# The grouped norm of a decoder trunk: summing squares onto all partitions with a matrix of ones, and taking the reciprocal root there

## The chip, the cores and the metric

The kernel runs on one core of a Trainium2 chip. The core has five engines that work side by side, each through its own instructions in order: TensorE (PE in the profile; its weight loads are a row of their own, PEld), VectorE (DVE), ScalarE (ACT), GpSimd (POOL) and SyncE (SP), which issues most of the DMAs. The metric is the device time of one execution in microseconds (us), the median of several runs.

## The reference

Two layers of a hybrid decoder, on a sequence of 256 tokens with 1024 channels in float32. Each layer normalises its input, makes one wide projection of it, and runs three token mixers on the parts: a Mamba-2 scan, a sliding-window attention and a forgetting attention. Each mixer has a SiLU gate; its result is projected back to 1024 channels, the three are merged with sigmoid gates, and an output projection is added to the stream.

The change touches the end of the Mamba branch, the grouped norm, which takes the mean of squares over each of 4 groups of 256 channels, per token:

```python
def grouped_rms_norm(y, w, groups):
    b, s, d = y.shape
    yf = y.astype(jnp.float32).reshape(b, s, groups, d // groups)
    yf = yf * lax.rsqrt(jnp.mean(yf * yf, axis=-1, keepdims=True) + NORM_EPS)
    return (yf.reshape(b, s, d) * w.astype(jnp.float32)).astype(y.dtype)

    y = y.reshape(b, s, SSM_INNER) * jax.nn.silu(z)     # the end of mamba2_branch
    return grouped_rms_norm(y, norm_w, SSM_GROUPS)
```

## The kernel before

**Layout.** In the Mamba branch the channels lie on the 128 partitions and the 256 tokens along the row. `y.xs` holds 8 such tiles of 128x256, so a group of the norm is two tiles, and its sum of squares runs over two tiles and all 128 partitions, for each of 256 columns.

**Products in two halves.** A large product is made with operands split into a high part, rounded to the matmul's fast float32r format, and the low rest: high times high, low times high and high times low are added in PSUM. The helper `split` (L291, L292) makes both parts: an ACT copy to the high part and a DVE subtraction for the low one. Every weight that arrives from memory goes through it as two pieces of 128x1024 a block (`hi`, `lo`), so DVE and ACT must keep ahead of PE with weights all the time. `AHEAD` pieces at most are held split.

**The order of work.** PE's order is written by hand: the kernel is recorded under a manual schedule for PE, unit after unit (a unit is one projection of 128 channels, or of 512 columns for one half of the tokens). After a unit, and at some points within, `pump` lets small generators, such as a norm group, take a step. A generator's step is due a given time after the last, by a planner's clock that counts matmuls (L101 to L110): `D_GN1` is 8.0 us from launch to the first visit to PE, `D_GN2` 13.5 us from there to the second. DVE, ACT and POOL get their order from a scheduler that follows dependencies and priorities; in the program that is built it is fixed. What is in the list `ends_later` is recorded behind the next eviction of a product out of PSUM (`finish`).

**The norm, before.** In `u_z` (L863 to L902) the gate of tile `u` is made (`gated`, L876 and L877) and multiplied in (L888); the tile is squared on ACT (L890). After each second tile the two squares are added (L893) and a generator `group_norm` is launched. It does, per group:

1. first visit to PE: the squares (two blocks of 128 tokens) as the weights and two columns of ones as the moving operand, so that the sums come out with the tokens on partitions: 4 used columns in PSUM;
2. on DVE `v`, mean and epsilon (L909, 128x4); on POOL the power -1/2 (L912, 128x4);
3. on DVE a Newton step in three operations (L917, L918, L920), and the split into high and low (L923, L924); on ACT four diagonal matrices, identity times the value of each token (L927);
4. second visit to PE: a matrix of ones times these diagonals, which leaves the value of each token on all partitions, 128x256 in PSUM;
5. for both tiles the product with the norm's weight and this value (L940), and its split into the operands of the projection (`y.yh`, `y.yl`).

**Around it.** While the four groups of a layer go through this, PE works on the last units of the gate, on value products of an attention (L676 evicts them), and on the 512-column sigmoid gates (L1022 evicts them). The branch's projection follows, whose first piece needs the first groups' results and whose second the last group's. POOL's next work behind the four powers is the merge of the projected branch (L1070).

The lines that the instructions of the norm carry in the changed kernel: square sum L894, `v` L914, power L915, Newton step L919 (twice) and L920, product L929.

Of the kernel before, what the change touches and what calls it, by code (L numbers as in the profile page):

```python
# [11 lines left out]
F32 = mybir.dt.float32  # L12
F32R = mybir.dt.float32r
AF = mybir.ActivationFunctionType
ALU = mybir.AluOpType

P = 128
S = 256
# [4 lines left out]
EPS = 1e-6  # L23
# [3 lines left out]
D_GN1, D_GN2, D_CUM, D_H, D_M = 8.0, 13.5, 12.0, (4.8, 6.4), 5.0  # L27
# [20 lines left out]
def hybrid_trunk(  # L48
# [5 lines left out]
    nc = tc.nc  # L54
# [11 lines left out]
    def T(tag, shape, dtype=F32, bufs=None):  # L66
        count[0] += 1
        return sb.tile(shape, dtype, tag=tag, name=f"{tag}_{count[0]}",
                       bufs=bufs if bufs is not None else BUFS.get(tag, 1))

    def PS(tag, bufs):
        count[0] += 1
        return ps.tile([P, 512], F32, tag=tag, name=f"{tag}_{count[0]}", bufs=bufs)
# [4 lines left out]
    def pmx():  # L78
        return PS("mx", 5)

    act = nc.scalar.activation
    stt = nc.vector.scalar_tensor_tensor
    tt = nc.vector.tensor_tensor
    ts = nc.vector.tensor_scalar
    gtt = nc.gpsimd.tensor_tensor
# [14 lines left out]
    def mm(o, a, b, **kw):  # L100
        n = b.free_size()  # L101
        if a.dtype == F32R:
            clock["t"] += max(0.094, n / 2350.0)
        else:
            clock["t"] += max(0.2, n / 587.0) * (0.5 if a.free_size() == 64 or a.shape[0] == 32 else 1.0)
        nc.tensor.matmul(o, a, b, **kw)  # L106
# [5 lines left out]
    def launch(br, gen, delay=0.0):  # L112
        clock["n"] += 1
        waiting.append([clock["t"] + delay, clock["n"], br, gen, None, False])
# [32 lines left out]
    def pump(budget=BUDGET):  # L147
        t0 = clock["t"]
        half = False
        while True:  # L150
            over = clock["t"] - t0 >= budget
            if over and not half:
                return
            for m in sorted(waiting, key=lambda m: (m[0], m[1])):
                if ready(m) and (m[5] if over else not early(m)):
                    half = m[5]
                    enter(m)
                    break
            else:
                return  # L160

    def drain(br):

        left = 0
        while any(m[2] == br for m in waiting):
            for m in sorted(waiting, key=lambda m: (m[0], m[1])):
                if m[2] == br and allowed(m):
                    left += 1
                    enter(m)
                    break  # L170
            else:
                m = min((m for m in waiting if allowed(m)), key=lambda m: (m[0], m[1]))
                left += 1
                enter(m)
        if left and VERBOSE:
            print("drained", br, left, "at", round(clock["t"], 1))
# [10 lines left out]
    ident = T("ident", [P, P])  # L187
# [11 lines left out]
    onesr = T("ones", [P, P], F32R)  # L199
    nc.gpsimd.tensor_copy(onesr, one)  # L200
    ones = onesr.bitcast(F32)
# [9 lines left out]
    mhalf = T("mhalf", [P, 8])  # L211
# [11 lines left out]
    def root(v, n):  # L223
        r0 = T("sm", [P, 8])
        nc.gpsimd.tensor_tensor(r0[:, :n], v[:, :n], mhalf[:, :n], op=ALU.pow)
        return r0
# [54 lines left out]
    def halves(ap):  # L281

        return ap.rearrange("p (a i) -> p a i", a=2)
# [4 lines left out]
    def split(hi, lo, src, scale=None, keep=lambda f: f):  # L288

        if scale is None:  # L290
            keep(act)(hi, src, AF.Copy)  # L291
            keep(tt)(lo, src, hi.bitcast(F32), op=ALU.subtract)  # L292
        else:
            keep(act)(hi, src, AF.Copy, scale=scale)
            keep(stt)(lo, src, scale, hi.bitcast(F32), op0=ALU.mult, op1=ALU.subtract)
# [130 lines left out]
    for l in range(L):  # L426
        y = Layer()
# [49 lines left out]
    def chan_sum(y, w, c, out):  # L477


        p = pmm()  # L480
        both_sums(y, w, c, p)
        finish(act(halves(out), ordered(p[:, S:2 * S]), AF.Copy))
        tt(halves(out), ordered(p[:, 0:S]), halves(out), op=ALU.add)

    def dma_sum(y, w, c, out):

        p = pmm()
        both_sums(y, w, c, p)
        lo = T("L1", [P, S])
        act(halves(lo), ordered(p[:, S:2 * S]), AF.Copy)  # L490
        last = act(halves(out), ordered(p[:, 0:S]), AF.Copy)  # L491
        nc.gpsimd.dma_start(out, lo, accum_op=ALU.add)  # L492
        finish(last)

    def after_evictions(n, f):

        ends_later.append(f if n == 1 else lambda: after_evictions(n - 1, f))
# [298 lines left out]
    ends_later = []  # L796
# [68 lines left out]
    def u_z(y, br, u, c):  # L865
        def f(w):
            if u == 0 and br != 0:
                y.sz[br] = T("L8", [P, NK, S])
            elif u == 0:
                y.yh[br] = T("L8", [P, 2, NK, P], F32R)  # L870
                y.yl[br] = T("L8", [P, 2, NK, P], F32R)
            o = T("L1", [P, S]) if br == 0 else y.sz[br][:, u, :]

            def gated():
                th = T("L1", [P, S])
                act(th, o, AF.Tanh, scale=0.5)  # L876
                stt(o, th, 1.0, o, op0=ALU.add, op1=ALU.mult)  # L877
                y.zdone.add((br, u))
            if br == 1:
                dma_sum(y, w, c, o)  # L880
                after_evictions(3, gated)
                pump()
                return
            chan_sum(y, w, c, o)

            def normed():
                gated()
                tt(y.xs[:, u, :], y.xs[:, u, :], o, op=ALU.mult)  # L888
                sq = T("L1", [P, S])
                act(sq, y.xs[:, u, :], AF.Square)  # L890
                y.sq.append(sq)
                if u % 2 == 1:
                    tt(y.sq[-2], y.sq[-2], y.sq[-1], op=ALU.add)  # L893
                    launch(3 if u < 4 else 4, group_norm(y, u // 2, y.sq[-2]), D_GN1)  # L894
            if br == 0:
                drain(0)

                ends_later.append(normed)
            else:
                gated()  # L900
            pump()
        return f  # L902

    def group_norm(y, g, q0):
        p = pmx()
        for t in range(2):
            mm(p[:, 2 * t:2 * t + 2], q0[:, t * P:(t + 1) * P], ones[:, 0:2], start=True, stop=True)
        v = T("sm", [P, 8])
        ts(v[:, 0:4], p[:, 0:4], 1.0 / 256, 4 * EPS, op0=ALU.mult, op1=ALU.add)  # L909

        r0 = T("sm", [P, 8])
        nc.gpsimd.tensor_tensor(r0[:, 0:4], v[:, 0:4], mhalf[:, 0:4], op=ALU.pow)  # L912
        rbs = [T("L1", [P, S], F32R) for _ in range(2)]

        def diagonals():  # L915
            a = T("sm", [P, 8])
            tt(a[:, 0:4], r0[:, 0:4], v[:, 0:4], op=ALU.mult)  # L917
            tt(a[:, 0:4], a[:, 0:4], r0[:, 0:4], op=ALU.mult)  # L918
            r = T("rs", [P, 8], bufs=4)  # L919
            stt(r[:, 0:4], a[:, 0:4], -3.0, r0[:, 0:4], op0=ALU.add, op1=ALU.mult)  # L920

            rh, rl = T("sm", [P, 8], F32R), T("sm", [P, 8])
            nc.vector.tensor_copy(rh[:, 0:4], r[:, 0:4])  # L923
            tt(rl[:, 0:4], r[:, 0:4], rh[:, 0:4].bitcast(F32), op=ALU.subtract)  # L924
            for rb, v_ in zip(rbs, (rh.bitcast(F32), rl)):
                for t in range(2):
                    act(rb[:, t * P:(t + 1) * P], ident, AF.Copy, scale=v_[:, 2 * t:2 * t + 1])  # L927


        ends_later.append(diagonals)  # L930
        yield D_GN2
        if diagonals in ends_later:
            ends_later.remove(diagonals)
            diagonals()
        p = pmx()
        for i, rb in enumerate(rbs):
            mm(p[:, 0:S], onesr, rb, start=(i == 0), stop=(i == 1))
        for u in (2 * g, 2 * g + 1):
            n = T("L1", [P, S])
            stt(n, y.xs[:, u, :], y.vec[:, 80 + u:81 + u], p[:, 0:S], op0=ALU.mult, op1=ALU.mult)  # L940
            split(y.yh[0][:, :, u, :], y.yl[0][:, :, u, :], halves(n))


# [255 lines left out]
    for y in layers:  # L1199
# [10 lines left out]
        def cols(c0, n=256):  # L1210
            return sub([(0, w[:, c0:c0 + n])], n)
# [39 lines left out]
        if l == 0:  # L1251
            v, cv0, cv1 = cols(C_BV), cols(C_CV), cols(C_CV + 256)
# [8 lines left out]
        else:  # L1261
            cv0, v = cols(C_CV, 512), cols(C_BV)
# [87 lines left out]
    with tc.manual_schedule(engines={ENG.PE, ENG.DVE, ENG.Activation, ENG.Pool}):  # L1350
# [11 lines left out]
        p = pmx()  # L1362
# [93 lines left out]
        for i in range(2):  # L1456
# [4 lines left out]
        v = T("sm", [P, 8])  # L1461
        nc.vector.tensor_reduce(v[:, 0:2], ss.rearrange("p (t j) -> p t j", t=2), axis=mybir.AxisListType.X,
                                op=ALU.add)
        ts(v[:, 0:2], v[:, 0:2], 1.0 / D, EPS, op0=ALU.mult, op1=ALU.add)
        r0 = root(v, 2)
# [48 lines left out]
```

## Time and profile before

| | |
|---|---|
| median of 3 runs | 821.57 us (821.18 to 821.93) |
| profiled execution | 820.72 us, its span 819.0 us |
| mean granted clock of TensorE | 0.999 |
| busy: PE / DVE / ACT / POOL | 808.4 / 671.5 / 547.6 / 172.6 us |
| first-layer norm | `v` of the first group at 297.0 us, last product L940 ends at 333 us |
| second-layer norm | last `v` at 719.5 us |

The span runs from the first instruction to the last in one execution that the hardware profiler recorded; the rest of the execution's time lies around it. A row of a group gives the line, engine, operation, what it writes and reads with shapes, how often, then total busy time and the mean of one in ns, then idle time of the engine before these instructions and what ended it. A row of the timeline gives start and duration in us, and in brackets the idle time before and who ended it. A row of the waits gives who waited for whom: total us, times, longest. A row of stages gives busy time of each engine in a window. The chain is followed back from the last instruction, at each step to what released it.

### The profile page before, as it was taken

What the parts mean: (1) busy time and instruction counts of PE and PEld (TensorE: products, weight loads), DVE (VectorE), ACT (ScalarE), POOL (GpSimd) and SP (SyncE); (2) the same over time, 40 slices, a digit from 0 to 9 for tenths busy, and PEclk for the clock granted to TensorE, in tenths of its full rate; (3) what the DMA queues carried; (4) which work ended last, traced back from release to release, by engine and by line L of the source; (5) the groups of instructions that cost most, each with busy time, mean ns of one, the idle gap of its engine ahead of it and who ended that gap; (6) DMA issues with size and microseconds to landing.
All of it is one profiled execution on the core that took longest, in us unless ns stands there. A gap on an engine that the chain in (4) does not pass through costs nothing.

```text
span 819.0 us, 15070 instructions
## 1 busy us (share of the span) xinstructions
PE 808.4 (99%) x5242; PEld 721.2 (88%) x5242; DVE 671.5 (82%) x1468; ACT 547.6 (67%) x1186; POOL 172.6 (21%) x232
## 2 busy tenths in 40 slices
PE   8999999999999999999999999999999999999996
PEld 8998988888888988888999898889888889888896
DVE  6879899888998787965786989988899878787665
ACT  7777878775776767543666777886567767684452
POOL 3066113130210001030005621314004210102100
PEclk9999999999999999999999999999999999999999
DMA  9897869797865554866689787869868565467632
GB/s 312 278 261 193 211 187 256 190 233 214 232 206 157 180 168 148 276 208 205 221 265 265 186 222 206 228 179 259 243 206 231 155 181 163 137 208 265 206 104 77
DMA packets 141653, 170.35 MB, mean 208 GB/s; under 512 B 9314, under 2 KB 110298, under 8 KB 141578
## 3 DMA queue, kind: packets, MB, share of 16 engines
q1 hardware_dynamic: 114960, 140.53, 54.8%
q0 software_dynamic: 12928, 12.63, 9.5%
q10 hardware_dynamic: 13690, 16.24, 6.5%
q8 instruction: 41, 0.67, 0.3%
q14 instruction: 34, 0.28, 0.1%
HBM read 154.63 MB, written 2.16 MB: 191 GB/s over the span
## 4 chain that ended last, share of the span: by engine, by line
PE 85%; DVE 4%; DMA 4%; ACT 4%; issue 2%; POOL 0%; SPq 0%; ACTq 0%; DVEq 0%; POOLq 0%
PE mm L106 75%; PE mx L106 7%; PE mx L110 3%; DMA L<-cumd 2%; DVE lo L292 1%; ACT hi L291 1%; DVE L L781 1%; ACT pp L621 1%; DMA L<-L 1%; DMA raw<-in_w_in_dram 1%; DMA bias<-cumd 1%; ACT L L778 0%; ACT L L490 0%; DVE L L830 0%; POOL bias L991 0%
## 5 line engine op out<-in xcount | busy, mean ns | idle before, releaser
L292 DVE TENSOR_TENSOR lo<-raw,hi 128x1024 fp32r<-128x1024 f32 (+2 forms) x276 | 310.5, 1144 | 53.2 <-ACT hi L291 50.5
L106 PE MATMUL mm<-L,hi 128*128 128x512 f32 x1056 | 353.2, 386 | 0.0
L106 PE MATMUL mm<-hi,L 128*128 128x512 f32 (+2 forms) x1232 | 323.3, 351 | 0.1
L291 ACT ACTIVATE hi<-raw 128x1024 fp32r<-128x1024 f32 (+2 forms) x276 | 263.9, 981 | 57.2 <-PE mm L106 45.2
L106 PE MATMUL mm<-L,lo 128*128 128x256 f32 x1056 | 266.6, 273 | 0.0
L106 PEld LDWEIGHTS mm<-hi,L 128*128 128x128 f32 x1232 | 216.9, 190 | 24.1 <-issue 1.3
L106 PEld LDWEIGHTS mm<-L,hi 128*128 128x128 f32 x1056 | 194.5, 190 | 26.4 <-issue 3.2
L106 PE MATMUL mm<-lo,L 128*128 128x512 f32 (+2 forms) x616 | 213.8, 349 | 1.8 <-DVE lo L292 1.8
L106 PEld LDWEIGHTS mm<-L,lo 128*128 128x128 f32 x1056 | 202.1, 191 | 5.5
L106 PEld LDWEIGHTS mm<-lo,L 128*128 128x128 f32 x616 | 116.3, 190 | 14.1 <-DVE lo L292 2.6
L492 POOL DMA_DIRECT2D L<-L x68 | 59.4, 925 | 184.5 <-ACT L L491 151.3
L621 ACT ACTIVATE pp<-pp,nm 128x128 f32<-128x128 f32 (+1 forms) x128 | 56.5, 442 | 30.8 <-DVE nm L615 30.7
L991 POOL TENSOR_SCALAR_AFFINE_SELECT bias<-bias 128x128 f32<-128x128 f32 x64 | 34.6, 592 | 93.5 <-DMA bias<-cumd 92.7
L781 DVE SCALAR_TENSOR_TENSOR L<-L,vec,L 128x255 f32<-128x255 f32 (+2 forms) x96 | 46.2, 481 | 2.2 <-ACT L L778 0.5
L490 ACT ACTIVATE L<-mm 128x256 f32<-128x256 f32 x84 | 31.6, 376 | 15.9 <-PE mm L106 14.2
L1025 ACT ACTIVATE L<-L 128x512 f32<-128x512 f32 x24 | 15.1, 629 | 31.6 <-DVE L L1022 27.2
L633 DVE TENSOR_SCALAR pp<-pp,rsum 128x128 f32<-128x128 f32 (+1 forms) x128 | 32.5, 319 | 0.5
L492 POOL DMA_DIRECT2D qt<-L x16 | 14.5, 990 | 81.9 <-ACT qt L491 40.4
L877 DVE SCALAR_TENSOR_TENSOR L<-L,L 128x256 f32<-128x256 f32 x48 | 21.4, 449 | 8.6 <-ACT L L876 8.3
L652 ACT ACTIVATE L<-mx 128x512 f32<-128x512 f32 x48 | 26.8, 595 | 1.5 <-PE mx L110 1.5
L1070 POOL TENSOR_TENSOR L<-L,L 128x512 f32<-128x512 f32 x8 | 12.8, 1598 | 68.4 <-DVE L L1069 68.4
L912 POOL TENSOR_TENSOR sm<-sm,mhalf 128x4 f32<-128x4 f32 x8 | 8.1, 1019 | 90.5 <-DVE sm L909 90.5
(197 smaller groups left out, 841.8 us busy)
## 6 DMA issues: line engine op xcount, KB each, us to landing
raw<-in_w_in_dram SPq DMA_DIRECT2D x191, 512.0 KB, 4.7
raw<-in_w_proj_dram SPq DMA_DIRECT2D x48, 512.0 KB, 5.3
L<-L POOLq DMA_DIRECT2D x72, 128.0 KB, 5.0
raw<-in_w_out_dram SPq DMA_DIRECT2D x16, 512.0 KB, 5.1
bias<-cumd ACTq DMA_DIRECT2D x16, 256.0 KB, 3.4
L<-cumd ACTq DMA_DIRECT2D x8, 512.0 KB, 5.9
L<-in_gate_bias_dram ACTq DMA_DIRECT2D x12, 256.0 KB, 5.9
qt<-L POOLq DMA_DIRECT2D x16, 128.0 KB, 5.6
```

What stands on the lines that cost most here:

```text
L106: nc.tensor.matmul(o, a, b, **kw)
L110: nc.tensor.transpose(o, a, i)
L291: keep(act)(hi, src, AF.Copy)
L292: keep(tt)(lo, src, hi.bitcast(F32), op=ALU.subtract)
L490: act(halves(lo), ordered(p[:, S:2 * S]), AF.Copy)
L492: nc.gpsimd.dma_start(out, lo, accum_op=ALU.add)
L621: act(pp[:, i, sl], pp[:, i, sl], AF.Exp, scale=-1.0, bias=nm[:, e:e + 1], accum_out=sums[:, e:e + 1])
L633: ts(pp[:, i, sl], pp[:, i, sl], rs[:, 2 * i + b:2 * i + b + 1], 0.5, op0=ALU.mult, op1=ALU.mult)
L652: act(pT, pt, AF.Copy)
L781: stt(a[:, s:S], x_[:, 0:S - s], y.vec[:, 16 * j + u:16 * j + u + 1], a[:, s:S], op0=ALU.mult, op1=ALU.add)
L877: stt(o, th, 1.0, o, op0=ALU.add, op1=ALU.mult)
L991: nc.gpsimd.affine_select(out=bias[:, i, dst], in_=bias[:, i, src], compare_op=ALU.is_ge, fill=NEG, base=0, pattern=[[-1, P]], channel_mul ...
```

## The change

The squares of a group are added as before, but the sum is then split into high and low parts (`parts_`). The first visit multiplies a matrix of ones as the weights by these two parts, so that the sum of each token comes out on all 128 partitions at once, 128x256. `v`, the power on POOL and the Newton step now work on 128x256 instead of 128x4; the exponent is one column, broadcast along the row. Diagonals and the second visit to PE are gone; the products with the norm's weight read the value from SBUF. The due times are unchanged.

```diff
                 if u % 2 == 1:
-                    tt(y.sq[-2], y.sq[-2], y.sq[-1], op=ALU.add)
-                    launch(3 if u < 4 else 4, group_norm(y, u // 2, y.sq[-2]), D_GN1)
+                    q = y.sq[-2]
+                    tt(q, q, y.sq[-1], op=ALU.add)
+                    parts_ = [T("L1", [P, S], F32R) for _ in range(2)]
+                    split(*parts_, q)
+                    launch(3 if u < 4 else 4, group_norm(y, u // 2, parts_), D_GN1)
...
-    def group_norm(y, g, q0):
+    def group_norm(y, g, parts_):
         p = pmx()
-        for t in range(2):
-            mm(p[:, 2 * t:2 * t + 2], q0[:, t * P:(t + 1) * P], ones[:, 0:2], start=True, stop=True)
-        v = T("sm", [P, 8])
-        ts(v[:, 0:4], p[:, 0:4], 1.0 / 256, 4 * EPS, op0=ALU.mult, op1=ALU.add)
-        r0 = T("sm", [P, 8])
-        nc.gpsimd.tensor_tensor(r0[:, 0:4], v[:, 0:4], mhalf[:, 0:4], op=ALU.pow)
-        rbs = [T("L1", [P, S], F32R) for _ in range(2)]
-        def diagonals():
-            a = T("sm", [P, 8])
-            tt(a[:, 0:4], r0[:, 0:4], v[:, 0:4], op=ALU.mult)
-            tt(a[:, 0:4], a[:, 0:4], r0[:, 0:4], op=ALU.mult)
-            r = T("rs", [P, 8], bufs=4)
-            stt(r[:, 0:4], a[:, 0:4], -3.0, r0[:, 0:4], op0=ALU.add, op1=ALU.mult)
-            rh, rl = T("sm", [P, 8], F32R), T("sm", [P, 8])
-            nc.vector.tensor_copy(rh[:, 0:4], r[:, 0:4])
-            tt(rl[:, 0:4], r[:, 0:4], rh[:, 0:4].bitcast(F32), op=ALU.subtract)
-            for rb, v_ in zip(rbs, (rh.bitcast(F32), rl)):
-                for t in range(2):
-                    act(rb[:, t * P:(t + 1) * P], ident, AF.Copy, scale=v_[:, 2 * t:2 * t + 1])
-        ends_later.append(diagonals)
+        for i, q in enumerate(parts_):
+            mm(p[:, 0:S], onesr, q, start=(i == 0), stop=(i == 1))
+        v, r = T("L1", [P, S]), T("L1", [P, S])
+        ts(v, p[:, 0:S], 1.0 / 256, 4 * EPS, op0=ALU.mult, op1=ALU.add)
+        gtt(r, v, mhalf[:, 0:1].to_broadcast([P, S]), op=ALU.pow)
+
+        def newton():
+            for _ in range(2):
+                tt(v, v, r, op=ALU.mult)
+            stt(r, v, -3.0, r, op0=ALU.add, op1=ALU.mult)
+
+        ends_later.append(newton)
         yield D_GN2
-        if diagonals in ends_later:
-            ends_later.remove(diagonals)
-            diagonals()
-        p = pmx()
-        for i, rb in enumerate(rbs):
-            mm(p[:, 0:S], onesr, rb, start=(i == 0), stop=(i == 1))
+        if newton in ends_later:
+            ends_later.remove(newton)
+            newton()
         for u in (2 * g, 2 * g + 1):
             n = T("L1", [P, S])
-            stt(n, y.xs[:, u, :], y.vec[:, 80 + u:81 + u], p[:, 0:S], op0=ALU.mult, op1=ALU.mult)
+            stt(n, y.xs[:, u, :], y.vec[:, 80 + u:81 + u], r, op0=ALU.mult, op1=ALU.mult)
             split(y.yh[0][:, :, u, :], y.yl[0][:, :, u, :], halves(n))
```

## The prediction

> **What bounds the kernel now.** I read the page first (busy shares, then the chain that ended last), then the busy time by stage around the grouped norm, then the waits, and last the single instructions of the norm on POOL, DVE and PE. The page:
>
> ```profile
> span 819.0 us, 15070 instructions
> ...
> PE 808.4 (99%) x5242; PEld 721.2 (88%) x5242; DVE 671.5 (82%) x1468; ACT 547.6 (67%) x1186; POOL 172.6 (21%) x232
> ...
> PE 85%; DVE 4%; DMA 4%; ACT 4%; issue 2%; POOL 0%; SPq 0%; ACTq 0%; DVEq 0%; POOLq 0%
> ```
>
> TensorE (PE) is the bound: busy 99%, and 85% of the chain. POOL is busy 21% and has no share of the chain. The stage of the first layer's norm, with its columns PE, weight loads, DVE, ACT, POOL, then clock and DMA:
>
> ```profile
> 297.00:327.00 30.00, 30.00 (x171) 26.05 (x170) 23.05 (x59) 21.15 (x47) 4.04 (x4) 1.00 0.50 159
> ```
>
> PE has no gap in these 30 us, DVE is idle for 7 of them. A matmul saved here shortens the run, and so does nothing else; but DVE feeds PE (it makes the `lo` half of every weight and adds the results out of PSUM), so a DVE that stands still stops PE some microseconds later. The waits between POOL and DVE in the norm, in total over both layers:
>
> ```profile
> POOL sm L912 <- DVE sm L909: 90.5, 6, 29.1
> ...
> DVE sm L917 <- POOL sm L912: 7.0, 6, 1.2
> ```
>
> The first row is POOL without work. The second is what matters: DVE already stands still for each power, 1.2 us at most, because the Newton step stands right behind it in DVE's order. Today PE does not feel it.
>
> **The change part by part.** *The power on POOL.* Four times a layer, the power (L912) on 128x4 becomes one on 128x256 with a broadcast exponent. No power that wide is in the trace. The powers that are:
>
> ```profile
> L912 POOL TENSOR_TENSOR sm<-sm,mhalf x8: 1001/1008/1056, 297.2 to 719.8; 128x4 f32<-128x4 f32 x8
> ...
> L258 POOL TENSOR_TENSOR sm<-sm,mhalf x2: 577/1024/1471, 404.0 to 414.6; 128x1 f32<-128x1 f32 x2
> ...
> L225 POOL TENSOR_TENSOR sm<-sm,mhalf x1: 713/713/713, 15.3 to 15.3; 128x2 f32<-128x2 f32 x1
> ```
>
> (min/median/max in ns.) One column takes 577 ns, two 713, four 1008: 136 ns more for the second column, 147.5 for each of the next two. A line through them is 430 ns and 144 ns a column, which at 256 columns is 37.3 us; by the two slopes, 1.008 + 252 x 0.136 = 35.3 and 1.008 + 252 x 0.1475 = 38.2 us. Against it stands the other single-column power, 1471 ns: with it the mean of one column is that of four, and one could say that the width costs nothing. And the same op slot with an addition or a subtraction:
>
> ```profile
> L1070 POOL TENSOR_TENSOR L<-L,L 128x512 f32<-128x512 f32 x8 | 12.8, 1598 | 68.4 <-DVE L L1069 68.4
> ...
> L565 POOL TENSOR_TENSOR L<-L,L 128x256 f32<-128x256 f32 x2 | 2.1, 1043 | 0.0
> ...
> L463 POOL TENSOR_SCALAR nega<-nega 128x16 f32<-128x16 f32 x2 | 0.7, 341 | 0.0
> ```
>
> So the ends are 1.04 us (the power as cheap as a subtraction) and 38.2 us. I take 37.3 because an ordinary POOL instruction of 16 columns costs 341 ns in all, and four columns of power cost three times that: something in the power is paid by the column. The eight four-column rows lie within 55 ns of each other, so the 1471 is the odd row.
>
> The Trainium skill speaks against this. "GPSIMD Engine Reference", section 3.1 (Elementwise — side-by-side cycle accounting), puts a two-input operation at about 2.6 cycles an element and 4497 ns for 2048. By that an estimate for 256 columns is near 1 us and the sum would be a gain. The trace agrees for additions (1598 - 1043 = 555 ns for 256 columns more), not for the power; the page times no power. It is the second rival below.
>
> *Who waits.* In DVE's built order of the changed kernel the Newton step's first multiplication (it needs the power) stands directly behind its `v` in the first two groups, and with three others between in the last two. DVE works in order: everything behind it waits. The next group's `v` stands behind the Newton step of the group before, so POOL cannot take the four powers one after the other either; DVE and POOL take turns. DVE's rows for the sum:
>
> ```profile
> 296.99 0.16 DVE L909 TENSOR_SCALAR sm<-mx 128x4 f32<-128x4 f32 x1
> 298.32 0.16 DVE L917 TENSOR_TENSOR sm<-sm,sm 128x4 f32<-128x4 f32 x1 [1.17 <-POOL sm L912]
> 298.40 1.23 DVE L292 TENSOR_TENSOR lo<-raw,hi 128x1024 fp32r<-128x1024 f32 x1
> 299.55 0.15 DVE L918 TENSOR_TENSOR sm<-sm,sm 128x4 f32<-128x4 f32 x1
> ...
> 299.81 0.42 DVE L483 TENSOR_TENSOR L<-mm,L 128x256 f32<-128x256 f32 x1
> 300.15 0.41 DVE L877 SCALAR_TENSOR_TENSOR L<-L,L 128x256 f32<-128x256 f32 x1
> ...
> 304.32 0.69 DVE L676 TENSOR_TENSOR L<-mm,L 128x512 f32<-128x512 f32 x1
> 304.92 1.22 DVE L292 TENSOR_TENSOR lo<-raw,hi 128x1024 fp32r<-128x1024 f32 x1
> 306.05 0.23 DVE L909 TENSOR_SCALAR sm<-mx 128x4 f32<-128x4 f32 x2
> ...
> 310.95 0.42 DVE L877 SCALAR_TENSOR_TENSOR L<-L,L 128x256 f32<-128x256 f32 x1 [1.00 <-ACT L L876]
> 311.41 0.42 DVE L888 TENSOR_TENSOR L<-L,L 128x256 f32<-128x256 f32 x1
> ```
>
> From start to start a 128x1024 `lo` takes 1.15 us, a 128x512 0.60, a 128x256 0.34, and 0.46 where it needs the one before it. A `v` of 128x256 takes 0.42. From `v` to the Newton step is therefore the power + 0.42 + 0.13 (today 298.32 - 296.99 = 1.33, less a power of 1.05 and 0.16). Between the waits stand, in the built order: from the first Newton step to the second `v` 15 instructions, two of 128x1024, two of 128x512 and eleven of 128x256, 2.3 + 1.2 + 3.86 = 7.4, and I take 7.7, which is what the same stretch takes now (298.32 to 306.05); from the second to the third `v` three of 128x1024, one of 128x512, seven of 128x256, 3.45 + 0.6 + 2.6 = 6.7, with 0.5 for waits on ACT 7.2; to the fourth seven of 128x256, 2.5. From the first `v` to the last Newton step: 4 x (37.3 + 0.55) + 7.7 + 7.2 + 2.5 = 168.8 us.
>
> *What PE has meanwhile.* The order written for PE lets it go on until it needs a `lo` that stands behind the last Newton step on DVE: the ninth matmul of the fifth 512-wide product after the square sums. Today:
>
> ```profile
> 324.92 0.59 PE L106 MATMUL mm<-hi,L 128*128 128x512 f32 x2
> ...
> 326.64 0.38 PE L106 MATMUL mm<-lo,L 128*128 128x512 f32 x1
> ```
>
> That product begins in the first row and its ninth matmul is the second, at 326.64. In the changed kernel the first `v` starts about 0.7 us later than now (two more 128x256 splits ahead of it), at 297.7; the last Newton step at 297.7 + 168.8 = 466.5; the `lo` is ready 1.6 us on, at 468.1. PE is late by 468.1 - 326.64 = 141.5 us. Then its next two parts come 1.5 us apart while PE eats one in 1.3: 0.5 more. 142 us a layer. PE has no idle time later in which to win it back. Layer 2 has the same order, and its rows are those of layer 1 some 402 us later:
>
> ```profile
> 708.12 0.22 DVE L909 TENSOR_SCALAR sm<-mx 128x4 f32<-128x4 f32 x2
> 709.47 0.16 DVE L917 TENSOR_TENSOR sm<-sm,sm 128x4 f32<-128x4 f32 x1 [1.13 <-POOL sm L912]
> ```
>
> *PE itself.* Chain rows of the visits, first and second:
>
> ```profile
> 293.07 0.34 PE mx L106 x4
> ...
> 304.90 0.79 PE mx L106 x8
> 305.69 2.70 PE mm L106 x12
> 308.39 0.24 PE mx L106 x2
> ...
> 316.39 0.34 PE mx L106 x4
> ...
> 319.43 0.47 PE mx L106 x4
> ```
>
> Removed per layer: first visits 0.34 + 0.79 + 0.34 = 1.47, second visits 0.24 + 0.47 and, for the fourth, as for the first 0.24 = 0.95. Added: four first visits of the kind that the second now is, 0.95. Net 1.47 a layer, 2.9 us in all. All of it lies inside the stretch in which PE now waits for DVE, so in my sum it is worth nothing; if that cover is gone it is worth 2.9.
>
> *DVE and ACT.* DVE gains per group a `lo` split, and six small operations of about 0.16 become four of 0.42: some 1.1 us. It is counted above. ACT loses four copies and gains one of 128x256:
>
> ```profile
> L291 ACT ACTIVATE L<-L 128x256 fp32r<-128x256 f32 x16 | 6.0, 400 | 0.0
> ...
> L927 ACT ACTIVATE L<-ident,sm 128x128 fp32r<-128x128 f32 x32 | 9.9, 387 | 0.0
> ```
>
> That is 1.1 us less a group. PE's cover hides both; without it DVE's 1.1 would be at most 9 us over eight groups. No DMA is added or moved past another on SP or POOL; on POOL nothing stands between the four powers, and what follows (L1070) is needed only after PE's projections. The L1 ring is turned twice more per group, which in this sum can only lengthen a wait that is there anyway.
>
> *The sum.* The profiled execution took 820.7 (span 819.0), 0.9 under the median of 821.57. 820.7 + 2 x 142 = 1104.7, say 1105.
>
> The Trainium skill has one thing that would lengthen it: "TensorE: Matmul & The Clock Gate", Part 1, halves the clock after an idle window of about 3.4 us and restores it after as long. The trace has no idle time of PE that long, so nothing here shows it. An estimate from it is 1.7 us at each resumption that lies on the path, one a layer, and the sum would be 1108.
>
> **The rivals.** *The column gets cheaper in a long row.* An inner loop could overlap columns, which one to four columns would not show. Against it: the slope rises from 136 to 147.5 and does not fall. At half the price the power takes 18.7 us, PE is late by 4 x (18.7 + 0.55) + 17.4 + 297.7 + 1.6 - 326.64 + 0.5 = 67.5 a layer, and the time is 956.
>
> *The other side: the power costs what a subtraction does.* For it: the 1471 row, and 1043 ns for 128x256. Then the DVE wait is what it is today, and PE's 2.9 us remain: 818. It decides where the four waits fit into PE's lead: 4 x (power + 0.55) + 17.4 + 1.6 + 297.7 = 326.64, a power of 1.9 us, 6 ns a column. Above it the kernel is slower. "GPSIMD Engine Reference", section 3.1, of the Trainium skill is the rule that would have it so.
>
> *The power is longer than the line.* A broadcast operand or a busy SBUF could stretch it as the 1471 row was stretched; at 45 us the time is 1105 + 8 x 7.7 = 1167.
>
> **How the numbers follow.** Full price by the column 0.76, a cheaper column 0.11, a cheap power 0.10, a longer one 0.03. Time: 1105. Within the first case the slopes give 35.3 to 38.2 us, 1089 to 1112, and with 5 us a layer for my stretches 1080 to 1122. The range goes down to half price, 955, which takes in half of the second case, and up to 1140 for part of the last: 0.82. A change of 0.2% (1.6 us) is about what can be told from none. Slower 0.88: the first, second and last cases without the few powers near 1.9 us; same 0.02; faster 0.10.
>
> **What would show it.** POOL rows of 128x256 at about 37 us, eight of them, 300 us of POOL; a wait of DVE's Newton step on POOL of some 290 us in eight times; PE busy near 73% of the span, with four gaps a layer between about 300 and 470 us; DVE and POOL in the chain that ended last where only PE stood. I am wrong if the wide power takes under 2 us, or if DVE's row behind `v` does not wait.

## The result, and the profile after

The changed kernel takes 1143.79 us in the median of four runs (1142.94 to 1145.28), the kernel before beside it 821.75 (821.18 to 821.97): 1.3929 times the time before (95% interval 1.3909 to 1.3949). The profiled execution took 1142.94 us. The direction and the mechanism are those of the prediction, but the time lies 39 us above the 1105 forecast and 4 us above the upper end of its range.

The page of the kernel after: its span, the busy shares, then PE and its granted clock in forty slices of 28.5 us, the chain that ended last, and the row of the power among the groups.

```profile
span 1141.2 us, 14978 instructions
...
PE 820.7 (72%) x5210; PEld 726.1 (64%) x5210; DVE 678.9 (59%) x1460; ACT 542.1 (48%) x1162; POOL 492.8 (43%) x232
...
PE   9999999999605030099999999999993133002997
...
PEclk9999999999857565599999999999997575655999
...
PE 52%; POOL 29%; DVE 9%; ACT 5%; issue 3%; DMA 2%; SPq 0%; ACTq 0%; POOLq 0%; DVEq 0%
...
L915 POOL TENSOR_TENSOR L<-L,mhalf 128x256 f32<-128x256 f32 x8 | 329.3, 41160 | 99.4 <-DVE L L914 83.5
```

PE does about the same work as before (820.7 us busy after 808.4), but in two stretches of the run, one a layer, it hardly works. POOL had no share of the chain before and has 29% now. Eight powers take 329.3 us; the span grew by 322.2. The waits, in total over both layers, with how often and the longest:

```profile
DVE L L919 <- POOL L L915: 325.3, 8, 41.4
...
PEld mm L106 <- DVE lo L292: 154.3, 4, 76.4
PE mm L106 <- DVE lo L292: 152.7, 4, 76.0
...
PE mm L106 <- ACT L L890: 83.3, 2, 41.6
...
PE mx L106 <- ACT L L291: 73.1, 2, 36.6
```

The first row is the cause, the PE rows its effect: the Newton step L919 stands in DVE's order, waits 40 us for each of eight powers, and everything behind it, above all the `lo` halves of the weights, waits too. PE's waits on ACT L890 and L291 have the same cause: those are squares and splits on ACT that themselves wait for DVE's work behind the Newton step (L888 and L894).

The four turns of the first layer, on POOL:

```profile
300.53 41.17 POOL L915 TENSOR_TENSOR L<-L,mhalf 128x256 f32<-128x256 f32 x1 [32.33 <-DVE L L914]
349.65 41.11 POOL L915 TENSOR_TENSOR L<-L,mhalf 128x256 f32<-128x256 f32 x1 [7.94 <-ACT L L890]
398.41 41.12 POOL L915 TENSOR_TENSOR L<-L,mhalf 128x256 f32<-128x256 f32 x1 [7.65 <-DVE L L914]
442.54 41.23 POOL L915 TENSOR_TENSOR L<-L,mhalf 128x256 f32<-128x256 f32 x1 [3.01 <-DVE L L914]
```

on DVE:

```profile
299.97 0.42 DVE L914 TENSOR_SCALAR L<-mx 128x256 f32<-128x256 f32 x1
341.74 0.89 DVE L919 TENSOR_TENSOR L<-L,L 128x256 f32<-128x256 f32 x2 [41.36 <-POOL L L915]
...
349.05 0.42 DVE L914 TENSOR_SCALAR L<-mx 128x256 f32<-128x256 f32 x1
390.80 0.42 DVE L919 TENSOR_TENSOR L<-L,L 128x256 f32<-128x256 f32 x1 [41.33 <-POOL L L915]
...
397.86 0.42 DVE L914 TENSOR_SCALAR L<-mx 128x256 f32<-128x256 f32 x1
...
439.57 0.43 DVE L919 TENSOR_TENSOR L<-L,L 128x256 f32<-128x256 f32 x1 [39.86 <-POOL L L915]
...
442.04 0.42 DVE L914 TENSOR_SCALAR L<-mx 128x256 f32<-128x256 f32 x1
...
483.80 0.42 DVE L919 TENSOR_TENSOR L<-L,L 128x256 f32<-128x256 f32 x1 [40.08 <-POOL L L915]
```

and PE where it resumes for good:

```profile
485.41 0.79 PE L106 MATMUL mm<-lo,L 128*128 128x512 f32 x1 [75.87 <-DVE lo L292]
486.00 1.06 PE L106 MATMUL mm<-hi,L 128*128 128x512 f32 x2
486.85 0.63 PE L106 MATMUL mm<-lo,L 128*128 128x512 f32 x1
487.27 1.06 PE L106 MATMUL mm<-hi,L 128*128 128x512 f32 x2
...
490.66 0.59 PE L106 MATMUL mm<-hi,L 128*128 128x512 f32 x2
491.09 0.38 PE L106 MATMUL mm<-lo,L 128*128 128x512 f32 x1
491.31 0.59 PE L106 MATMUL mm<-hi,L 128*128 128x512 f32 x2
```

POOL and DVE take turns, as forecast: a power, 2.5 to 7.3 us of DVE, the next power. PE resumes at 485.41, 1.6 us after the last Newton step has its power. It first runs at half speed: two `hi` matmuls and a `lo` take 1.27 us (486.00 to 487.27), and 0.65 later (490.66 to 491.31). The stages show the clock (columns PE, weight loads, DVE, ACT, POOL, then clock, DMA share and GB/s):

```profile
443.00:484.00 41.00, 0.00 (x0) 0.00 (x0) 0.93 (x3) 3.97 (x5) 40.76 (x1) 0.50 0.03 6
484.00:489.80 5.80, 4.39 (x10) 3.52 (x11) 5.80 (x10) 0.87 (x3) 0.00 (x0) 0.50 0.47 151
490.00:500.00 10.00, 10.00 (x48) 8.74 (x47) 10.00 (x16) 5.47 (x9) 0.00 (x0) 0.99 0.74 209
```

The granted clock is 0.50 through the pause and for at least 4.4 us of work behind it (485.41 to 489.80). That stretch is not fixed: in a second profile of the same kernel it lasts at least 5.7 us.

### The profile page after: what moved, and what is told of

Its sections match the earlier page's. It is cut to its first block, busy times and chain, and to the rows that moved or that the text cites. A ratio compares the mean times of both kernels' runs of the same rounds, so it can differ in the third digit from the quotient of the medians.

```text
span 1141.2 us, 14978 instructions
## 1 busy us (share of the span) xinstructions
PE 820.7 (72%) x5210; PEld 726.1 (64%) x5210; DVE 678.9 (59%) x1460; ACT 542.1 (48%) x1162; POOL 492.8 (43%) x232
## 4 chain that ended last, share of the span: by engine, by line
PE 52%; POOL 29%; DVE 9%; ACT 5%; issue 3%; DMA 2%; SPq 0%; ACTq 0%; POOLq 0%; DVEq 0%
PE mm L106 46%; POOL L L915 29%; PE mx L106 4%; DVE lo L292 3%; PE mx L110 2%; ACT hi L291 1%; ACT pp L621 1%; DMA L<-L 1%; DVE L L781 1%; DMA L<-cumd 0%; DVE L L676 0%; DMA raw<-in_w_in_dram 0%; ACT L L876 0%; ACT L L778 0%; ACT L L652 0%
## 5 line engine op out<-in xcount | busy, mean ns | idle before, releaser
L915 POOL TENSOR_TENSOR L<-L,mhalf 128x256 f32<-128x256 f32 x8 | 329.3, 41160 | 99.4 <-DVE L L914 83.5
L106 PE MATMUL mm<-hi,L 128*128 128x512 f32 (+2 forms) x1232 | 330.3, 357 | 0.1
L106 PE MATMUL mm<-lo,L 128*128 128x512 f32 (+2 forms) x616 | 217.7, 355 | 152.7 <-DVE lo L292 152.7
L291 ACT ACTIVATE hi<-raw 128x1024 fp32r<-128x1024 f32 (+2 forms) x276 | 263.6, 981 | 57.3 <-PE mm L106 46.2
L106 PEld LDWEIGHTS mm<-hi,L 128*128 128x128 f32 x1232 | 222.1, 194 | 26.7 <-issue 1.8
L919 DVE TENSOR_TENSOR L<-L,L 128x256 f32<-128x256 f32 x16 | 6.8, 422 | 325.4 <-POOL L L915 325.3
L1014 ACT ACTIVATE L<-L 128x512 f32<-128x512 f32 x24 | 15.1, 629 | 186.3 <-DVE L L1011 182.0
L106 PE MATMUL mm<-L,L 128*64 128x256 f32 (+1 forms) x64 | 8.6, 429 | 83.3 <-ACT L L890 83.3
L291 ACT ACTIVATE L<-L 128x256 fp32r<-128x256 f32 (+1 forms) x44 | 20.6, 504 | 93.7 <-DVE L L929 85.2
L106 PE MATMUL mx<-L,ones 128*128 128x256 f32 (+2 forms) x24 | 6.2, 334 | 75.1 <-ACT L L291 73.1
L106 PEld LDWEIGHTS mm<-L,L 128*64 128x64 f32 x64 | 5.7, 180 | 85.6 <-ACT L L890 83.7
L106 PEld LDWEIGHTS mx<-L,ones 128*128 128x128 f32 (+1 forms) x24 | 4.5, 205 | 77.1 <-ACT L L291 73.9
L492 POOL DMA_DIRECT2D qt<-L x16 | 14.6, 942 | 81.9 <-ACT qt L491 44.9
```

What stands on the lines that cost most here:

```text
L915: gtt(r, v, mhalf[:, 0:1].to_broadcast([P, S]), op=ALU.pow)
L919: tt(v, v, r, op=ALU.mult)
L1014: finish(act(g, g, AF.Tanh, scale=0.5))
```

## The experiments

The theory under test: eight serial waits of DVE on POOL make the whole loss, and their length is a price by the column. The rivals: a price that falls in long rows, or one that depends on the broadcast exponent, on the values or on a busy SBUF; the half clock or the layout of the norm as a cost of its own.

**The price of a power by its width.** A kernel of its own, with powers and multiplications on POOL alone. Each is made three times; the inner loop for that is not shown, and the line numbers at the right are those in the profile.

```diff
+    for n in (1, 2, 4, 8, 16, 32, 64, 128, 256):
+        gtt(r[:, 0:n], v[:, 0:n], mh[:, 0:n], op=ALU.pow)                          # L74
+    for n in (1, 4, 64, 256):
+        gtt(r[:, 0:n], v[:, 0:n], mh[:, 0:1].to_broadcast([P, n]), op=ALU.pow)     # L77
+    for n in (64, 256):
+        gtt(r[:, 0:n], one[:, 0:n], mh[:, 0:n], op=ALU.pow)                        # L80
+        gtt(r[:, 0:n], wide[:, 0:n], mh[:, 0:n], op=ALU.pow)                       # L83
+    for n in (4, 64, 256):
+        gtt(r[:, 0:n], v[:, 0:n], mh[:, 0:n], op=ALU.mult)                         # L86
```

> A kernel of its own, which leaves the whole trunk out: it loads x, does powers on POOL one after the other, each three times, and stores x. Widths 1, 2, 4, 8, 16, 32, 64, 128 and 256 with a full tile of exponents; 1, 4, 64 and 256 with one broadcast exponent; 64 and 256 with all ones as values and with squares spread over many orders of magnitude; 4, 64 and 256 with a multiplication. In the changed kernel the power took 41.16 us where the line through one, two and four columns (430 ns + 144 ns a column) gave 37.3. Theory 'the price of a column settles higher than the first four show': full exponents and broadcast both give 41.1 at 256, and the step per column rises from about 144 ns to 159 by 16 columns. Rival 'broadcast exponent': full exponents give 37.3 at 256 and the broadcast ones 41.1. Rival 'values': 256 columns of ones differ from 256 spread ones by over 1 us. Rival of the prediction that stays to be buried, 'a long row gets cheaper': the step falls with width.

The groups of this kernel, each with its total and the mean of one in ns:

```profile
L74 POOL TENSOR_TENSOR r<-v,mh 128x256 f32<-128x256 f32 x3 | 123.7, 41226 | 0.2
L80 POOL TENSOR_TENSOR r<-one,mh 128x256 f32<-128x256 f32 x3 | 123.7, 41226 | 0.2
L83 POOL TENSOR_TENSOR r<-wide,mh 128x256 f32<-128x256 f32 x3 | 123.7, 41226 | 0.2
L77 POOL TENSOR_TENSOR r<-v,mh 128x256 f32<-128x256 f32 x3 | 123.4, 41118 | 0.2
L74 POOL TENSOR_TENSOR r<-v,mh 128x128 f32<-128x128 f32 x3 | 62.3, 20773 | 0.2
L74 POOL TENSOR_TENSOR r<-v,mh 128x64 f32<-128x64 f32 x3 | 31.6, 10544 | 0.2
...
L74 POOL TENSOR_TENSOR r<-v,mh 128x16 f32<-128x16 f32 x3 | 8.7, 2899 | 0.2
L74 POOL TENSOR_TENSOR r<-v,mh 128x8 f32<-128x8 f32 x3 | 4.9, 1635 | 0.2
...
L74 POOL TENSOR_TENSOR r<-v,mh 128x4 f32<-128x4 f32 x3 | 3.0, 1007 | 0.2
L86 POOL TENSOR_TENSOR r<-v,mh 128x256 f32<-128x256 f32 x3 | 2.2, 722 | 0.2
L74 POOL TENSOR_TENSOR r<-v,mh 128x2 f32<-128x2 f32 x3 | 2.1, 700 | 0.2
L74 POOL TENSOR_TENSOR r<-v,mh 128x1 f32<-128x1 f32 x3 | 1.7, 561 | 4.0 <-DVE v L67 3.9
```

On an otherwise idle core the wide power with a broadcast exponent takes 41.12 us, and 41.16 in the kernel, so a busy SBUF is not in it. A broadcast exponent (L77), ones as values (L80) and widely spread values (L83) change it by 0.3% at most. The price of one more column rises: 139 ns for the second, 153 from two to four, 157 from four to eight, 158 from eight to sixteen, 160 from 64 to 128 and from 128 to 256. It settles at about 0.16 us a column, so no short row of the kernel before shows it in full; why it rises was not tried. A multiplication of the same width takes 0.72 us: it is the power that costs, not the row.

**The same kernel with a multiplication in place of the power.** The norm's reciprocal root is left out.

```diff
-        gtt(r, v, mhalf[:, 0:1].to_broadcast([P, S]), op=ALU.pow)
+        gtt(r, v, mhalf[:, 0:1].to_broadcast([P, S]), op=ALU.mult)
```

> The changed kernel with the power replaced by a multiplication of the same shape and operands, so the norm's value is left wrong and all else is as it is. Theory (the whole loss is the time of the power): POOL's instruction takes about 1.0 us, DVE waits about 1.1 us for it as before, and PE is spared 2.9 us: 818 us, 0.4% under the kernel before. Rival 'the wide operations on DVE and the two splits more per group cost by themselves': 822 to 829 us, DVE's 1.1 us a group on the path.

It took 820.61 us beside 820.93 before: ratio 0.9998 (0.9987 to 1.0008). So the power is the whole loss, and all else in the change comes, in sum, to nothing that can be told from none. Neither number expected came out: the gain to 818 us is missing, and so is the loss to 822 or more. The group of the multiplication, PE's row at the gap in question, and the waits:

```profile
L915 POOL TENSOR_TENSOR L<-L,mhalf 128x256 f32<-128x256 f32 x8 | 5.1, 641 | 100.6 <-DVE L L914 84.7 <-PE mm L106 15.9
```

```profile
305.98 1.52 PE L106 MATMUL mm<-L,L 128*64 128x256 f32 x16 [1.07 <-ACT L L890]
```

```profile
PE mm L106 <- ACT L L890: 2.1, 2, 1.1
```

PE is busy 806.6 us, 1.8 less than before. Two new gaps of 1.1 us make about as much. The profile puts each down to a square on ACT (L890), which waits for DVE's L888; the chain in front of the first one runs through the multiplication on POOL, the Newton step and a `lo` on DVE.

**Half the columns, and 32 of them.** The power on part of the row and a multiplication on the rest, which leaves the reciprocal root out there: 128 columns of power in the first kernel, and `h = 32` with the other `S - h` columns multiplied in the second. The first edit:

```diff
-        gtt(r, v, mhalf[:, 0:1].to_broadcast([P, S]), op=ALU.pow)
+        h = S // 2
+        gtt(r[:, 0:h], v[:, 0:h], mhalf[:, 0:1].to_broadcast([P, h]), op=ALU.pow)
+        gtt(r[:, h:S], v[:, h:S], mhalf[:, 0:1].to_broadcast([P, h]), op=ALU.mult)
```

> The changed kernel with the power on the first 128 columns and a multiplication on the other 128, so half of the norm's values are left wrong. Theory (four waits one after the other, each as long as POOL's work): POOL takes 0.43 + 128 x 0.159 + 0.75 = 21.5 us, 19.6 less than 41.16, eight times: 1143 - 157 = 986 us. Rival 'part of the loss does not depend on the power's length' (cold PE, refilling, clock) does not move it from this slope, but the next run would then lie above its line. Rival 'waits overlap in part': less than 157 us gained.

> The same with the power on 32 columns and a multiplication on 224. POOL takes 0.43 + 32 x 0.159 + 1.0 = 6.5 us. Theory: by the prediction's sum with the first v where it was measured, 299.97 + 4 x (6.5 + 0.55) + 17.4 + 1.6 - 326.64 + 0.5 = 21 us a layer, 863 us; on the straight line from the changed kernel it would be 1143 - 8 x 34.7 = 865. Rival 'PE's lead covers short waits': near 820 to 830 us. Rival 'fixed loss at each pause of PE': over 875 us.

They took 981.99 us (1.1958 times before, 1.1936 to 1.1980) and 861.75 us (1.0494, 1.0475 to 1.0513), close to the 986 and 863 of the theory. POOL's group rows of the first and then of the second kernel:

```profile
L916 POOL TENSOR_TENSOR L<-L,mhalf 128x128 f32<-128x128 f32 x8 | 166.1, 20760 | 99.7 <-DVE L L914 83.8 <-ACT L L890 15.9
L917 POOL TENSOR_TENSOR L<-L,mhalf 128x128 f32<-128x128 f32 x8 | 3.2, 395 | 0.0
```

```profile
L916 POOL TENSOR_TENSOR L<-L,mhalf 128x32 f32<-128x32 f32 x8 | 43.7, 5457 | 99.4 <-DVE L L914 83.5 <-ACT L L890 15.9
L917 POOL TENSOR_TENSOR L<-L,mhalf 128x224 f32<-128x224 f32 x8 | 4.4, 556 | 0.0
```

Each group holds POOL for 41.2, 21.2, 6.0 and 0.64 us in the four kernels (all columns, 128, 32, none), and the times are 1143.8, 982.0, 861.75 and 820.6. Per microsecond of POOL that is (1143.8 - 982.0) / 20.0 = 8.1, then 120.2 / 15.1 = 7.9 and 41.1 / 5.4 = 7.7: close to eight, one for each wait, down to a few microseconds. PE's lead takes up almost nothing. Carried on at 7.7 to 8 a microsecond from the third kernel, the time before would be reached at 0.7 to 0.9 us of POOL (an estimate; no run lies between 0.64 and 6.0), not at the 1.9 us of the prediction.

**The four powers without the turns.** The Newton steps are taken out of `ends_later` and recorded at the generator's second step, which comes 40 us after the first visit by the planner's clock in place of 13.5, and both multiplications of each are pinned to their places behind other work of DVE.

```diff
-D_GN1, D_GN2, ... = 8.0, 13.5, ...
+D_GN1, D_GN2, ... = 8.0, 40.0, ...
...
-                tt(v, v, r, op=ALU.mult)
+                pin(tt)(v, v, r, op=ALU.mult)
...
-        ends_later.append(newton)
         yield D_GN2
-        if newton in ends_later:
-            ends_later.remove(newton)
-            newton()
+        newton()
```

> The changed kernel with the Newton steps recorded later: not behind the next eviction but at the generator's second step, whose due time is 40 us instead of 13.5, the first multiplication kept behind everything recorded on DVE before it. All four v then stand ahead of the first Newton step on DVE, and PE has work up to the branch's projection. Theory 'DVE in order hands the wait on, and DVE and POOL take turns': POOL's four powers follow each other without a gap, the last ends 4 x 41.2 us after the first begins, near 465 us, and PE stands at the projection's second half until about 470 instead of 342: 130 us a layer, about 1081 us. Rival 'the gaps between the powers do not matter, PE makes them good': 1143 us. Rival 'it is DVE's wait alone': far under 1081, since DVE no longer waits.

It took 1079.32 us: 1.3157 times before (1.3129 to 1.3185). POOL's row, and then PE's long gaps:

```profile
301.17 164.45 POOL L915 TENSOR_TENSOR L<-L,mhalf 128x256 f32<-128x256 f32 x4 [32.27 <-DVE L L914]
```

```profile
427.65 0.79 PE L106 MATMUL mm<-hi,L 128*128 128x512 f32 x1 [92.73 <-ACT L L291]
...
468.03 0.80 PE L106 MATMUL mm<-hi,L 128*128 128x512 f32 x1 [29.52 <-ACT L L291]
```

Now the powers stand back to back and end at 465.62, 18.2 us before those of the changed kernel (483.77), and PE has done more of its other work meanwhile (43.9 us busy from the start of the first power to the end of the last, 29.9 in the changed kernel). From the end of the last power to the next layer's first norm on POOL (L258) it is 68.5 us here (534.16 - 465.62) and 81.2 in the changed kernel (564.93 - 483.77). 18.2 + 12.6 = 30.8 a layer: this is the part of the loss, 64 of 322 us, that the place of the Newton step makes. For the rest, 164.5 us of powers stand without a gap between a layer's gate and its projection, and PE's two long gaps end 3.1 and 2.4 us behind the third and the fourth of them. With PE's order as it is, another order on DVE could hide little of that; whether other work of PE could be moved into the gaps was not tried.

**The clock kept up through the pause.** Spare matmuls, whose result nobody reads, stand in PE's order ahead of the third branch's first sigmoid gate, the product that stops in the long gap.

```diff
+            if br == 2 and c == 0 and t == 0:
+                spare = pmx()
+                for _ in range(340):                      # 314 in the second kernel
+                    nc.tensor.matmul(spare, onesr, y.hTh[:, 0, 0:4, :], start=True, stop=True)
             p = tok(y.hTh, y.hTl, w, t)
```

> The changed kernel with 340 matmuls of 128x512 more in each layer, whose result nobody reads, in PE's order directly ahead of the product at which PE stands still for DVE until the last Newton step. They fill 73 of the 76 us of that pause. Theory 'the half clock after a pause costs time': in the changed kernel the granted clock stands at 0.50 from the pause to about 489.8 us, and the first 4.4 us of work take 2.1 us longer than at full clock; kept busy, PE resumes at full clock and the run is 2 x 2.1 = 4.2 us shorter, about 1139 us. Rival 'PE is held by DVE's pieces there, not by its clock': no difference within 1 us. Rival 'the added matmuls run over': longer than the changed kernel.

It took 1146.56 us (1.3980, 1.3948 to 1.4011). The 340 took 79.5 us and ended after the `lo` was ready, so they were late themselves; nothing follows from this run. With 314, beside a second run of the changed kernel:

> The run before filled the pause with 340 matmuls, and they took 79.5 us instead of 73, because the first of them ran at half clock themselves; they ended at 489.5 us, 2.8 us after the piece that PE waited for was there (486.75). Now 314: they should end near 483.9 us, the eight matmuls ahead of the awaited piece 1.7 us later, and PE waits for about 1 us. Theory 'the half clock after the pause costs 2.1 us a layer': granted clock 1.00 from 486 us on, and 4.2 us less than the changed kernel of the same call, ratio to it 0.9963. Rival 'DVE's pieces hold PE there anyway': within 1 us of it, because the pieces behind come 1.5 us apart.

> The changed kernel as it is, for the comparison on the same chip: 1143.8 us by the first result.

1143.85 us (1140.62 to 1144.88) and 1143.17 (1142.13 to 1145.24): ratios to before 1.3913 (1.3885 to 1.3941) and 1.3907 (1.3884 to 1.3930). One thing in the expectation was wrong: the spare matmuls did not run at half clock; in the stages from 410 to 480 us the clock was 1.00, and each took 0.234 us (46.83 / 200 below). The stage in the kernel with 314, and its PE, the last 200 spare matmuls and the resumption:

```profile
484.00:489.80 5.80, 4.12 (x18) 3.04 (x17) 3.38 (x6) 0.00 (x0) 2.38 (x1) 1.00 0.06 18
```

```profile
437.80 46.83 PE L1011 MATMUL mx<-L,ones 128*128 128x512 f32 x200
...
488.03 0.48 PE L106 MATMUL mm<-lo,L 128*128 128x512 f32 x1 [1.68 <-DVE lo L292]
488.35 0.59 PE L106 MATMUL mm<-hi,L 128*128 128x512 f32 x2
```

At full clock from the start, the time is the same within what these runs tell; the 4.2 us of the theory are not there. From the end of the last power to the next layer's L258 it is 80.8 us here, 81.2 and 81.9 in the two profiles of the changed kernel. Over both layers, from the start of the first power to the end of the span, it is 839.9 us here, 840.7 and 841.7 there. The half clock is real, but in these profiles at most about a microsecond a layer of it reaches the end.

## Why the prediction was right, and where it was wrong

The sum of the prediction beside what the first layer's rows give; the last column is for both layers.

| step of the prediction | forecast, us | measured, us | over the run |
|---|---|---|---|
| the power on POOL | 37.3 | 41.16 | 8 x 3.86 = +30.9 |
| first `v` | 297.7 | 299.97 | +4.5 |
| first `v` to last Newton step, less four powers | 19.6 | 183.83 - 164.63 = 19.2 | -0.8 |
| from there to the `lo` that PE needs | 1.6 | 1.6 | 0 |
| behind the resumption | 0.5 | 79.52 - 77.39 = 2.1 | +3.3 |

(79.52 and 77.39 run from PE's matmul in question, at 485.41 and 326.64, to L258 of the next layer, at 564.93 and 404.03.) 1104.7 + 37.9 = 1142.6; the profiled execution took 1142.94. The second layer is like the first: up to that L258 the changed kernel's span is 160.9 us longer than before, behind it 161.3.

- **The power on POOL** is the step that failed, by its size. That a power is paid by the column was right, and so was setting the 1471 ns row aside: the same instruction takes 1.46 to 1.48 us in other profiles of this record (575.60 us in the changed kernel), where one column alone takes 0.56. What holds it up there is open. The 144 ns a column, from rows of one, two and four columns, was 10% too low: at 256 columns it is 159.8. The prediction saw the step rise from 136 to 147.5, and used that only against the rival of a cheaper column; the same rise spoke for a price above both slopes. It took the larger of the two slopes as the upper end (38.2 us); even the step from two to four columns is still below that of a long row (153 and 160 ns alone on POOL). Over eight serial waits 3.9 us are 31 us of the miss of 38. The first `v` and the work behind the resumption, both put too low, make the other 7.
- **Who waits** was right to the microsecond: the turns of POOL and DVE (7.3, 7.1 and 2.5 us between; forecast 7.7, 7.2, 2.5), the product in which PE stops for good, the 1.6 us to the `lo`. PE stops three times a layer for long (41.6, 36.5 and 75.9 us), not four: between the third and the fourth power DVE gets to only 2.5 us of work, and none of it lets PE go on.
- **First `v`** came 3.0 us later than before, not 0.7. It was later with a multiplication in place of the power too (301.26), so the work of DVE ahead of it does it and not the wait. Between the square sum at 289.8 us and `v` DVE's rows have, beside the two splits that the prediction counted (0.34 each), one 128x1024 `lo` more than before (three, 1.15 each) and 0.9 us more of waits on ACT.
- **PE itself, DVE and ACT**, taken as worth nothing under the pause, cannot be seen there. Without the pause (multiplication) PE's saving, 1.8 us busy and not 2.9, does not come through: 820.6 where the cheap-power rival gave 818. That rival's break-even, a power of 1.9 us, was too high as well: it gave PE's whole lead to the four waits, but `v` starts later and DVE has more to do.
- **The rivals.** The long row that gets cheaper is excluded by the widths. The longer power came nearest in its number, but not for the reasons that it named: neither the broadcast nor a busy SBUF adds anything.
- **The clock.** The clock does fall to 0.50 in the pause, and came back no sooner than 4.4 us after the resumption in one profile and 5.7 in the other. The Trainium skill ("TensorE: Matmul & The Clock Gate", Part 1) has at least one busy window of about 3.4 us for it, and the estimate from it was 1.7 us a layer. Both stretches here are longer than that window, and the table's last row has 1.6 us more than forecast. But with the clock held up, at most about 1 us a layer came back, so the closeness of 1.6 and 1.7 shows no cause. What else is in the 2.1 us stays open; DVE is busy without a pause in the first 9.6 us behind the resumption.
- **The page's price for POOL.** "GPSIMD Engine Reference", section 3.1, of the Trainium skill has 4497 ns for an addition of 2048 elements, which makes 0.56 us for 256, an estimate; the prediction's "near 1" was too high. The multiplication here comes near it, with 0.72 us alone and 0.64 in the kernel. The power does not: it takes 57 times the multiplication.

The signs named ahead stand: eight 128x256 rows on POOL (329 us, forecast 300), DVE waiting 325 us in eight times (forecast 290), PE at 72% (forecast 73%), POOL and DVE in the chain; the gaps of PE were three a layer, not the four named.

Nothing in the runs points to a version of this form that beats the kernel before: even with a nearly free operation in place of the power the time is the same.

## What to carry to other kernels

Where a price by the column rises over the few widths that a trace shows, a fit through the narrow rows should count as a low value and the range should reach further up than the steepest of them: here the fit was 10% short. A row near the width in use is worth more than any fit. Replicating a value onto all partitions before an operation that is paid by the column multiplies that operation, here from 4 columns to 256; it is the cheap operations that should come after the spreading. And before a slow operation goes to an engine that seems idle, look at what stands behind its consumer in order: here each microsecond of it came back as nearly eight, one for each of the eight powers, because DVE held the weights' splits behind the Newton step.

## What the hardware showed unasked

- POOL's power takes about 0.36 + 0.16 us a column from four columns up (1.01 us at 4, 10.5 at 64, 41.2 at 256), the same for ones, for widely spread values and with a broadcast exponent. A multiplication of 256 columns takes 0.72 us.
- PE's granted clock stood at 0.50 in the pauses and, behind the longest one, for at least 4.4 us of work in one profile and 5.7 in another of the same kernel. Keeping it up through the longest pause of each layer changed the run's time by less than could be measured.
- 128x512 matmuls into one PSUM tile with the same weights followed each other in 0.234 us at full clock, where the kernel's own products need 0.65 for three (0.217 each). Why was not tried.
